# Expert weights loaded as two neighbouring rows per partition, with the contraction order permuted to match

## The chip, the cores and the metric

The kernel runs on one core of one Trainium2 chip. The metric is the device time of one execution in microseconds. Three runs of the kernel before took 1764.06, 1769.62 and 1772.02 us; the median is 1769.62 us.

## What is computed

Two layers of a diffusion block over 256 latent tokens and 256 context tokens of 1024 channels. Each layer is a dense part (RMSNorm, attention, convolution and pooling branches, gates, output projection) and then an expert part, which is what the change touches:

```python
def expert_choice_ffn(h, w_router, w_gate, w_up, w_down):
    B, N, _ = h.shape
    cap = (CAPACITY_FACTOR * N) // N_EXPERTS          # 32 tokens per expert
    aff = jax.nn.softmax(jnp.einsum('bnd,de->bne', h, w_router).astype(F32), axis=-1)
    g, idx = lax.top_k(jnp.transpose(aff, (0, 2, 1)), cap)
    xe = h[bidx, idx]
    a = jnp.einsum('becd,edf->becf', xe, w_gate)
    u = jnp.einsum('becd,edf->becf', xe, w_up)
    ye = jnp.einsum('becf,efd->becd', jax.nn.silu(a) * u, w_down) * g[..., None].astype(h.dtype)
    return jnp.zeros_like(h).at[bidx, idx].add(ye)
```

There are 16 experts per layer, each with three matrices of 1024 x 1024 in float32 (12 MB per expert, 192 MB per layer). Layer 0 runs the experts for both token sets, layer 1 for the latent tokens alone.

## The kernel before

A weight matrix of an expert comes in four tiles of 1 MB, each with 256 rows of the matrix, on 128 partitions: `t[p, k, :]` holds row `128 k + p` of the 256 (line 334, in `prefetch`). Each partition so gets two rows of 4 KB that lie 128 rows apart in memory. The last expert's down matrix is loaded in another cut: four tiles of 512 rows by half of the columns, in runs of 2 KB. `prefetch` takes the next tile of a fixed list (gate and up in turn, then down, expert by expert) and a free buffer from a fixed rotation (`slot`: 15 buffers in layer 0, 19 in layer 1, most of them taken over from the dense part), and issues the load on SP's DMA queue. All large weights go through that queue in program order; small operands such as the router's weights, 1024 runs of 64 bytes (line 839), go through ACT's queue.

The rows of a tile stand on the partitions, so that TensorE contracts over them: tile column `kk` of tile `i` needs the chosen tokens' features `128 k` to `128 k + 127`, with `k = 2 i + kk`. These come on the partitions by `gather` (line 988), a product of the tokens with a selection matrix in which 128 columns of the residual `XS` are the stationary operand. For the down product, the hidden values `hs` are transposed in the same chunks of 128 columns (line 1094). The router uses the same feature order: line 896 transposes `XS`, line 839 loads `w_router`, and the scale and shift (`A2`, `modT`) are transposed at lines 168 and 248.

Per expert, TensorE runs 64 instructions of gate and up (line 1079), the transposes of the hidden values (line 1094) and 32 of down (lines 1103 and 1108); every four experts (two in layer 1) follow the products that add the results back to the residual (line 1125).

In layer 1 the router's weights are issued at the end of the dense part, beside the first expert tiles that fill free buffers; line 842 scales them on GpSimd, and line 888 is the first product that uses them. What stands behind line 888 on TensorE waits with it.

Of the kernel before, what the change touches and what calls it, by code (L numbers as in the profile page):

```python
# [23 lines left out]
EPS = 1e-6  # L24
# per layer: conv taps issued per step of a section; engine of the low part of a split (v: DVE, p: GpSimd);
# engine that scales a head's probabilities; units per chunk of the modulation products
TAPS = dict(attn=(1, 4), pool=(4, 0), merge0=(8, 1), merge2=(9, 18))
# [11 lines left out]
def const_tables():  # L39
    """Tables that depend on shapes alone."""  # L40
    f = np.float32
    kc = np.zeros((128, KC_END), f)
    p = np.arange(128)
    kc[:, KC_ID:KC_ID + 128] = np.eye(128, dtype=f)
    kc[p ^ 16, KC_PERM + p] = 1.0
    kc[:, KC_U:KC_U + 128] = (p[:, None] <= p[None, :])
    kc[:, KC_MA:KC_MA + 128] = np.where(p[None, :] > p[:, None], f(-1e30), f(0))
    kc[:, KC_MB:KC_MB + 128] = np.where(p[None, :] < p[:, None], f(-1e30), f(0))
    kc[:, KC_IOTA:KC_IOTA + 32] = np.arange(1, 33)
    kc[:, KC_SCOL] = p % 32 + 1  # L50
    t = np.arange(SEQ)
    for g, w in enumerate(POOLW):
        cnt = np.clip(t + w - w // 2, 0, SEQ) - np.clip(t - w // 2, 0, SEQ)
        r = (f(w) / cnt.astype(f)).astype(f)
        kc[:, KC_EDGE + 16 * g:KC_EDGE + 16 * g + 8] = r[:8]
        kc[:, KC_EDGE + 16 * g + 8:KC_EDGE + 16 * g + 16] = r[-8:]
    row, col = (t // 64).astype(f), (t % 64).astype(f)
    fr = (f(10000.0) ** (-np.arange(16, dtype=f) / f(16))).astype(f)
    rope = np.zeros((128, 2, SEQ), f)
    for q in range(128):  # L60
        d = q % 64
        ang = (row if d < 32 else col) * fr[d % 16]
        sgn = f(-1.0) if (d // 16) % 2 == 0 else f(1.0)
        rope[q, 0] = np.cos(ang)
        rope[q, 1] = sgn * np.sin(ang)
    return kc, rope.reshape(128, 2 * SEQ)


@with_exitstack
def dit_block(ctx: ExitStack, tc: tile.TileContext, out, kc_in, rope_in, x, c, ctx_in, c_ctx,  # L70
# [38 lines left out]

# [1 line left out]
    gps = open_psum("psd0", mm=3, md=1, ax=4)  # L111
# [8 lines left out]
    ident = kc[:, KC_ID:KC_ID + 128]  # L120
    NV = 64
    misc = L.tile([128, 2048], F32, tag="ws", name="misc", bufs=2)
    kt = misc[:, 512:512 + KC_END - KC_U]
    vrow, crow = misc[0:NV, 0:128], misc[0:16, 128:256]

    def rows(ap):
# [3 lines left out]
    nc.sync.dma_start(crow[8:16], c_ctx.rearrange("(k p) -> k p", p=128))  # L130
    VN1, VN2, VCB, VLG, VLB, VPS = 0, 16, 32, 40, 48, 56
    nc.gpsimd.dma_start(kt, kc_in[:, KC_U:KC_END])
# [5 lines left out]
    tokens(0)  # L138
    for o, ap in ((VN1, norm1_g), (VN2, norm2_g), (VCB, conv_dw_b), (VLG, conv_ln_g),
                  (VLB, conv_ln_b), (VPS, pool_scale)):  # L140
        r = rows(ap)
        nc.sync.dma_start(vrow[o:o + r.shape[0]], r)
# [15 lines left out]
    ucat = P0.tile([128, 3, 128], BF16, name="ucat")  # L158
    vec = P0.tile([128, NV], F32, name="vec")

    def small_operands():
        pv2 = bank("ax")
        nc.vector.tensor_copy(identb, ident)
        nc.vector.tensor_copy(maskb, kt[:, KC_MA - KC_U:KC_MA - KC_U + 256].rearrange("p (a b) -> p a b", a=2))
        nc.vector.memset(ucat[:, 0, :], 0.0)
        nc.vector.tensor_copy(ucat[:, 1, :], kt[:, 0:128])
        nc.vector.memset(ucat[:, 2, :], 1.0)
        nc.tensor.transpose(pv2[:, 0:NV], vrow, ident[:NV, :NV])
        nc.vector.tensor_copy(vec, pv2[:, 0:NV])

# [8 lines left out]
    def rms_scale(ss, n):  # L179
        """(ss / DM + EPS) ** -0.5"""  # L180
        r = small([128, 2], "rstd")
# [4 lines left out]
    for l in range(DEPTH):  # L186
# [3 lines left out]

        # ================= dense part =================
        if l:
# [23 lines left out]
        def mod_group(ll, g):  # L216
# [30 lines left out]
            for b in range(4):  # L247
                nc.tensor.transpose(pt[:, b * 128:(b + 1) * 128], mr[:, b * 128:(b + 1) * 128], ident)
            ptv = pt.rearrange("p (b j s m) -> p s j b m", b=4, j=4, s=2)
# [38 lines left out]

# [1 line left out]
        order = ["x0", "x1", "x2", "x3"]  # L290
# [32 lines left out]
        def prefetch(n):  # L323
            for _ in range(n):
                w_e, e, i = next(seq)
                t = slot("we")
                if w_e is w_e_down and e == NE - 1:
                    h, kq = i // 2, i % 2
                    t = t.rearrange("p (k n) -> p k n", k=4)
                    src = w_e[l, e, 512 * kq:512 * (kq + 1), 512 * h:512 * (h + 1)]  # L330
                else:
                    t = t.rearrange("p (k n) -> p k n", k=2)
                    src = w_e[l, e, 256 * i:256 * (i + 1), :]
                nc.sync.dma_start(t, src.rearrange("(k p) n -> p k n", p=128))
                ahead.append(t)
# [5 lines left out]

# [1 line left out]
        xn = [half(f"A{s}", "xn").rearrange("p (t d) -> p t d", t=2) for s in range(2)]  # L343
# [12 lines left out]
        def mod_first(hf, tag):  # L356
            """shift and scale of the first norm, feature blocks 4 hf .. 4 hf + 3"""
            ps = bank(tag)
# [80 lines left out]
        def pump_mod(n=1):  # L439
            """advance the remaining modulation products by n chunks"""  # L440
            while n > 0:
# [33 lines left out]
        def mm3(ps, w, a, nk, n):  # L475
            """ps += w.T @ a over nk chunks of 128, each operand in two exact parts"""
            (wh, wl), (ah, al) = w, a
# [19 lines left out]

# [1 line left out]
        QS = DR.tile([128, NH, 256], F32R, tag="qf", name="QS")  # L499
# [17 lines left out]
        for u in range(2):  # L517
            tv = qw.pop() if qw else qload(u)
            for v in range(2):
# [5 lines left out]
                if NS == 2:  # L525
                    nc.scalar.activation(qx[:, 256:512], ps[:, 256:512], AF.Copy)
                # each head's rows: the leading part, and the rest on the other 64 partitions
                for kv in range(2):
# [28 lines left out]

# [1 line left out]
        def branch(name):  # L559
# [41 lines left out]
        def weigh(s, kv, pT, pr4, rs):  # L601
            """normalised probabilities, keys on the partitions"""
            nk = 4 if s == 0 else 2
# [31 lines left out]

# [1 line left out]
        W = 256 + 2 * CPAD  # L637
# [44 lines left out]

# [1 line left out]
        wp = DR.tile([128, 4, 128], F32, tag="k2", name="wp")  # L684
# [32 lines left out]

# [1 line left out]
        m = [half(f"A{i}", "m") for i in range(NS)]  # L719
# [46 lines left out]
        for g in range(4):  # L766
# [6 lines left out]
                                           op1=ALU.subtract)  # L773
# [1 line left out]
        def conv_norm():  # L775
# [51 lines left out]

        # ================= output projection, router, top-k =================
        tail[0] = True
# [8 lines left out]
        nc.gpsimd.memset(wr, 0.0)  # L838
        nc.scalar.dma_start(wr[:, :, 0:NE], w_router[l].rearrange("(k p) e -> p k e", p=128))
        wra = rt_[:, 256:256 + 256 * NS].rearrange("p (s k e) -> p s k e", s=NS, k=8)  # L840
# [44 lines left out]
        def route(s):  # L885
# [5 lines left out]
            for d2 in range(4):  # L891
                pt = bank("ax")
                for dd in range(2):
                    for t in range(2):
                        d = 2 * d2 + dd
                        nc.tensor.transpose(pt[:, dd * 256 + t * 128:dd * 256 + t * 128 + 128],
                                            XS[s][:, t, d * 128:(d + 1) * 128], ident)
                xT = t2("xT")
# [79 lines left out]

# [1 line left out]
        def gather(s, parts):  # L980
            ne = NE // parts
            for part in range(parts):
                es = slice(ne * part, ne * part + ne)
                for d in range(8):
                    px = bank("mm")[:, :32 * ne]
                    for t in range(2):
                        Sv = St[s][:, t, es].rearrange("p e c -> p (e c)")
                        nc.tensor.matmul(px, XS[s][:, t, d * 128:(d + 1) * 128], Sv, start=t == 0,  # L988
                                         stop=t == 1)
                    pxv = px.rearrange("p (e c) -> p e c", e=ne)  # L990
# [36 lines left out]

        # ================= experts =================
        GE = 4 if NS == 2 else 2
        REP = 128 // GE  # L1030
        nsq = [small([128, 2, 2], "nsq") for _ in range(NS)]
        for e in range(NE):
# [3 lines left out]
            if e % GE == GE - 1:  # L1036
                # scatter matrices of the group: (expert, slot) by token, scaled by the affinity
                sgs = []
# [25 lines left out]

            # gate and up: column tiles of the array side by side
            nb = 2 if NS == 2 else 1
# [24 lines left out]
            for f in range(nb):  # L1091
                for q in range(4):
                    o = 256 * f + 64 * q
                    nc.tensor.transpose(pt[:, o:o + 64], hs[f][0:64, 128 * q:128 * q + 128],  # L1094
                                        ident[0:64, 0:64])
            hT = t2("hT")
# [106 lines left out]
```

## Time and profile before

| | |
|---|---|
| median of 3 runs | 1769.62 us |
| profiled execution, first to last instruction (span) | 1765.2 us |
| time of the profiled execution beside its span | the page lists none; its span stands within the three runs |
| TensorE busy | 1537.8 us (87%) |
| VectorE, ScalarE, GpSimd busy | 668.7, 407.7, 236.1 us |
| moved by DMA | 529.94 MB, mean 300 GB/s |
| SP's DMA queue | 179472 packets, 526.25 MB, 78.4% of 16 engines' span |
| expert loads | 3 x 128 transfers of 1024 KB |

The page cuts the span into 40 slices of 44.1 us. A packet is what one DMA engine moves in one piece: one contiguous run, at most. The share of a queue is the time that its packets took, over 16 engines and the span; over 100% means that packets of one engine overlap a little. TensorE's busy time is modelled, so a high share does not show that it sets the pace.

### The profile page before, as it was taken

The numbers are of one execution on the slowest core, as the hardware profiler recorded it, in microseconds if no ns is written. First come the engines' busy times: TensorE is split into PE (matmuls) and PEld (weight loads), VectorE is DVE, ScalarE is ACT, GpSimd is POOL, SyncE is SP. The second block draws the span as 40 slices with busy tenths as digits, with TensorE's granted clock in tenths as the row PEclk, the third lists the DMA queues.
The fourth block names the chain that finished last, engine by engine and source line by source line (L and its number), as shares of the span: only waits on it lengthen the run. The fifth ranks groups of instructions, "written<-read, shape, count | busy, mean of one in ns | idle before, by whom it ended". The sixth has DMA issues, their size and how long they took to land.

```text
span 1765.2 us, 19600 instructions
## 1 busy us (share of the span) xinstructions
PE 1537.8 (87%) x7792; PEld 809.1 (46%) x7792; DVE 668.7 (38%) x1144; ACT 407.7 (23%) x760; POOL 236.1 (13%) x242
## 2 busy tenths in 40 slices
PE   5999989999989999898899899999978766667676
PEld 2665566888654433232333267789742111111111
DVE  2568993452551221121211278965532110111011
ACT  2455312232431100000000157434421000000001
POOL 1300430154730000000000020225100000000000
PEclk9999999999999999999999999999989888888888
DMA  9733536254638999999999845666799999999996
GB/s 307 270 126 127 166 108 232 78 180 146 218 120 334 409 409 409 408 409 409 409 409 409 319 178 173 215 232 207 297 364 409 409 409 409 409 409 409 409 409 248
DMA packets 184331, 529.94 MB, mean 300 GB/s; under 512 B 11768, under 2 KB 60352, under 8 KB 179120
## 3 DMA queue, kind: packets, MB, share of 16 engines
q1 hardware_dynamic: 179472, 526.25, 78.4%
q10 hardware_dynamic: 4096, 1.97, 0.4%
q8 instruction: 61, 1.00, 0.2%
q0 software_dynamic: 672, 0.47, 0.1%
q14 instruction: 30, 0.25, 0.0%
HBM read 527.60 MB, written 1.05 MB: 299 GB/s over the span
## 4 chain that ended last, share of the span: by engine, by line
PE 37%; DMA 27%; DVE 5%; ACT 2%; POOL 2%; issue 1%; SPq 0%; POOLq 0%; ACTq 0%; DVEq 0%
DMA we<-in_w_e_up_dram 22%; PE mm L1079 11%; PE mm L1103 5%; DMA we<-in_w_e_down_dram 3%; PE mm L1108 3%; PE mm L480 2%; PE mm L988 2%; PE mm L479 2%; PE mm L482 2%; PE ax L1125 2%; PE mm L873 2%; DMA rt<-in_w_router_dram 1%; DVE hm L1086 1%; DVE acc L461 1%; PE ax L1094 1%
## 5 line engine op out<-in xcount | busy, mean ns | idle before, releaser
L1079 PE MATMUL mm<-we,xeT 128*64 128x512 f32 (+1 forms) x2048 | 445.9, 656 | 95.6 <-DMA we<-in_w_e_up_dram 75.3
L1079 PEld LDWEIGHTS mm<-we,xeT 128*64 128x64 f32 (+1 forms) x2048 | 126.6, 129 | 405.6 <-issue 201.1
L479 PE MATMUL mm<-hh,ws 128*128 128x512 f32 (+1 forms) x672 | 223.3, 351 | 1.4 <-ACT hh L413 1.2
L480 PE MATMUL mm<-hl,ws 128*128 128x512 f32 (+1 forms) x672 | 220.8, 347 | 0.0
L1086 DVE TENSOR_TENSOR hm<-si,mm 64x512 f32<-64x512 f32 x48 | 33.1, 690 | 468.1 <-ACT si L1084 467.2
L212 ACT ACTIVATE ws<-w 128x1024 fp32r<-128x1024 f32 x132 | 139.1, 1057 | 273.3 <-PE mm L482 186.2
L1084 ACT ACTIVATE si<-mm 64x512 f32<-64x512 f32 x48 | 28.4, 591 | 751.1 <-PE mm L1079 751.1
L461 DVE SCALAR_TENSOR_TENSOR acc<-up,dw,acc 128x512 f32<-128x512 f32 (+1 forms) x240 | 154.5, 687 | 0.9
L213 DVE TENSOR_TENSOR ws<-w,ws 128x1024 fp32r<-128x1024 f32 x94 | 123.6, 1319 | 71.9 <-ACT ws L212 71.5
L479 PEld LDWEIGHTS mm<-hh,ws 128*128 128x128 f32 x672 | 129.1, 193 | 31.5 <-issue 10.7
L480 PEld LDWEIGHTS mm<-hl,ws 128*128 128x128 f32 x672 | 129.2, 193 | 18.1 <-DVE hl L414 2.4
L1103 PE MATMUL mm<-we,hT 128*64 128x512 f32 x512 | 128.8, 635 | 8.4 <-ACT hT L1098 8.4
L482 PE MATMUL mm<-hh,ws 128*128 128x512 f32 (+1 forms) x672 | 134.8, 341 | 0.5 <-DVE ws L213 0.4
L213 POOL TENSOR_TENSOR ws<-w,ws 128x1024 fp32r<-128x1024 f32 x38 | 96.2, 2537 | 213.4 <-ACT ws L212 177.5
L482 PEld LDWEIGHTS mm<-hh,ws 128*128 128x128 f32 x672 | 107.6, 190 | 17.7 <-issue 2.4
L1044 POOL COPY sg<-kc 48x128 f32<-48x128 f32 (+1 forms) x16 | 4.4, 286 | 774.6 <-PE ax L1125 773.5
L1108 PE MATMUL mm<-we,hT 128*32 128x512 f32 x512 | 87.5, 790 | 11.9 <-DMA we<-in_w_e_down_dram 8.2
L1115 DVE TENSOR_TENSOR Y<-mm,G 32x512 f32<-32x512 f32 x64 | 44.0, 687 | 138.5 <-PE mm L1103 137.8
L1103 PEld LDWEIGHTS mm<-we,hT 128*64 128x64 f32 x512 | 39.2, 145 | 88.5 <-issue 75.1
L1125 PE MATMUL ax<-Y,sg 128*128 128x512 f32 x128 | 60.6, 619 | 8.8 <-DVE Y L1118 6.4
L1118 DVE TENSOR_TENSOR Y<-mm,G 64x512 f32<-64x512 f32 x32 | 22.0, 689 | 91.9 <-PE mm L1108 91.5
L749 POOL TENSOR_TENSOR m<-m,th 128x512 f32<-128x512 f32 (+1 forms) x32 | 36.6, 1143 | 145.1 <-DVE th L747 145.0
(271 smaller groups left out, 1594.6 us busy)
## 6 DMA issues: line engine op xcount, KB each, us to landing
we<-in_w_e_gate_dram SPq DMA_DIRECT2D x128, 1024.0 KB, 18.2
we<-in_w_e_up_dram SPq DMA_DIRECT2D x128, 1024.0 KB, 18.3
we<-in_w_e_down_dram SPq DMA_DIRECT2D x128, 1024.0 KB, 18.3
w<-in_w_mod_dram SPq DMA_DIRECT2D x40, 1024.0 KB, 5.0
w<-in_w_in_dram SPq DMA_DIRECT2D x38, 1024.0 KB, 5.2
w<-in_w_out_dram SPq DMA_DIRECT2D x12, 1024.0 KB, 5.1
w<-in_w_mod_dram SPq DMA_DIRECT2D x16, 512.0 KB, 10.8
w<-in_w_in_dram SPq DMA_DIRECT2D x8, 512.0 KB, 12.1
```

What stands on the lines that cost most here:

```text
L212: nc.scalar.activation(h, src, AF.Copy)
L213: (nc.gpsimd if eng == "p" else nc.vector).tensor_sub(lw, src, h.bitcast(F32))
L461: nc.vector.scalar_tensor_tensor(acc[:, ch], up[:, ch, :, k:k + 256], dw[:, 4 * k + ch:4 * k + ch + 1], acc[:, ch], op0=ALU.mult, op1=ALU.add)
L479: nc.tensor.matmul(ps, wh[:, k, :], ah[:, k, :n], start=k == 0, stop=False)
L480: nc.tensor.matmul(ps, wh[:, k, :], al[:, k, :n], start=False, stop=False)
L482: nc.tensor.matmul(ps, wl[:, k, :], ah[:, k, :n], start=False, stop=k == nk - 1)
L1079: nc.tensor.matmul(o, xeT[k // 4][:, k % 4, e, :], w[:, kk, 512 * f:512 * f + 512], start=k == 0, stop=k == 7)
L1086: nc.vector.tensor_mul(hm[0:64, :], si[0:64, :], pgu[f][64:128, :])
L1103: nc.tensor.matmul(pd[64 * h:64 * h + 64, :], hT[:, 64 * k:64 * k + 64], rhs, start=k == 0, stop=k == 7)
L1108: nc.tensor.matmul(pd[o:o + 32, :], hT[:, c0:c0 + 32], rhs, start=k < 2, stop=k >= 6)
L1115: nc.vector.tensor_mul(Y[b0:b0 + 32, s, cols], pd[rw, :], G2[l][rw, :])
L1125: nc.tensor.matmul(po, sgs[s][:, t * 128:(t + 1) * 128], Y[:, s, cols], start=True, stop=True)
```

## The change

Tile `t` of an expert's matrix now holds rows `2 p` and `2 p + 1` of its 256 rows on partition `p`: one run of 8 KB per partition, contiguous in memory and in the buffer, and the whole tile is 1 MB in one piece. Chunk `c` of 128 features is then no longer the columns `128 c` to `128 c + 127`, but every second column of a block of 256 (`paired(c)`), and all that meets such a chunk follows: the gathers, the router's transposes and weights, the transposes of the hidden values, and the scale, shift and gain of the second norm. These read their 128 columns with a step of two elements. The last expert's down matrix keeps its runs of 2 KB and is issued as eight loads of 512 KB instead of four of 1 MB. The router's weights are issued as two loads instead of one, with the same 1024 runs of 64 bytes.

```diff
+def paired(c):
+    return slice(256 * (c // 2) + c % 2, 256 * (c // 2) + 256, 2)
...
-    NV = 64
+    NV = 48
...
+    n2row = misc[0:8, 256:512]
...
+    nc.sync.dma_start(n2row, norm2_g.rearrange("l (i c) -> (l i) c", c=256))
...
-        nc.vector.tensor_copy(vec, pv2[:, 0:NV])
+        for kk in range(2):
+            nc.tensor.transpose(pv2[:, NV + 8 * kk:NV + 8 * kk + 8], n2row[:, paired(kk)], ident[:8, :8])
+        nc.vector.tensor_copy(vec[:, 0:NV], pv2[:, 0:NV])
+        nc.vector.tensor_copy(vec[:, VN2:VN2 + 16].rearrange("p (i k) -> p k i", k=2),
+                              pv2[:, NV:NV + 16].rearrange("p (k i) -> p k i", k=2))
...
             for b in range(4):
-                nc.tensor.transpose(pt[:, b * 128:(b + 1) * 128], mr[:, b * 128:(b + 1) * 128], ident)
+                cols = paired(b) if g else slice(b * 128, (b + 1) * 128)
+                nc.tensor.transpose(pt[:, b * 128:(b + 1) * 128], mr[:, cols], ident)
...
                 if w_e is w_e_down and e == NE - 1:
                     h, kq = i // 2, i % 2
                     t = t.rearrange("p (k n) -> p k n", k=4)
-                    src = w_e[l, e, 512 * kq:512 * (kq + 1), 512 * h:512 * (h + 1)]
+                    for ii in range(2):
+                        r0 = 512 * kq + 256 * ii
+                        nc.sync.dma_start(t[:, 2 * ii:2 * ii + 2], w_e[
+                            l, e, r0:r0 + 256, 512 * h:512 * (h + 1)].rearrange("(p k) n -> p k n", k=2))
                 else:
                     t = t.rearrange("p (k n) -> p k n", k=2)
-                    src = w_e[l, e, 256 * i:256 * (i + 1), :]
-                nc.sync.dma_start(t, src.rearrange("(k p) n -> p k n", p=128))
+                    nc.sync.dma_start(t, w_e[l, e, 256 * i:256 * (i + 1), :].rearrange(
+                        "(p k) n -> p k n", k=2))
...
-        nc.scalar.dma_start(wr[:, :, 0:NE], w_router[l].rearrange("(k p) e -> p k e", p=128))
+        for kk in range(2):
+            nc.scalar.dma_start(wr[:, kk::2, 0:NE], w_router[l].rearrange(
+                "(i p k) e -> p k i e", p=128, k=2)[:, kk])
...
-                                            XS[s][:, t, d * 128:(d + 1) * 128], ident)
+                                            XS[s][:, t, paired(d)], ident)
...
-                        nc.tensor.matmul(px, XS[s][:, t, d * 128:(d + 1) * 128], Sv, start=t == 0,
-                                         stop=t == 1)
+                        nc.tensor.matmul(px, XS[s][:, t, paired(d)], Sv, start=t == 0, stop=t == 1)
...
-                    nc.tensor.transpose(pt[:, o:o + 64], hs[f][0:64, 128 * q:128 * q + 128],
-                                        ident[0:64, 0:64])
+                    nc.tensor.transpose(pt[:, o:o + 64], hs[f][0:64, paired(q)], ident[0:64, 0:64])
```

SP's queue at the end of layer 1, where the last expert's tiles are issued (`we` is an expert tile, `xo` the result). Before:

```order
L334 DMA we<-in_w_e_gate_dram 128x2x1024
L334 DMA we<-in_w_e_up_dram 128x2x1024
L334 DMA we<-in_w_e_down_dram 128x4x512 x4
L1172 DMA out_dram<-xo 128x512 x4
L1199 UNCONDITIONAL_BRANCH
```

and changed:

```order
L348 DMA we<-in_w_e_gate_dram 128x2048
L348 DMA we<-in_w_e_up_dram 128x2048
L344 DMA we<-in_w_e_down_dram 128x2x512 x8
L1187 DMA out_dram<-xo 128x512 x4
L1214 UNCONDITIONAL_BRANCH
```

The order of the tiles is the same all through; a gate, up or down tile is one run per partition, and the last down matrix takes eight issues.

ScalarE's queue in layer 1 at the end of the dense part (`mh` is the leading half of the merged branches, `rt` the router's weights, `gb` a gate, `ws` a split weight). Before:

```order
L823 ACTIVATE mh<-m 128x256 x4
L839 DMA rt<-in_w_router_dram 128x8x16
L855 ACTIVATE gb<-ax 128x512 x2
L212 ACTIVATE ws<-w 128x1024 x4
L881 ACTIVATE junk,ssq<-xr 128x512
```

and changed:

```order
L838 ACTIVATE mh<-m 128x256 x4
L855 DMA rt<-in_w_router_dram 128x4x16 x2
L872 ACTIVATE gb<-ax 128x512 x2
L223 ACTIVATE ws<-w 128x1024 x4
L898 ACTIVATE junk,ssq<-xr 128x512
```

Here the two router loads stand together in the place of the one. In layer 0 the second of them stands behind one split (line 223) and one tanh (line 750).

## Rows read from the trace of the kernel before

**Rows 1.** The page: DMA's busy tenths and rate in 40 slices.
```profile
DMA  9733536254638999999999845666799999999996
GB/s 307 270 126 127 166 108 232 78 180 146 218 120 334 409 409 409 408 409 409 409 409 409 319 178 173 215 232 207 297 364 409 409 409 409 409 409 409 409 409 248
```
**Rows 2.** The page: the chain that ended last, by line.
```profile
DMA we<-in_w_e_up_dram 22%; PE mm L1079 11%; PE mm L1103 5%; DMA we<-in_w_e_down_dram 3%; PE mm L1108 3%; PE mm L480 2%; PE mm L988 2%; PE mm L479 2%; PE mm L482 2%; PE ax L1125 2%; PE mm L873 2%; DMA rt<-in_w_router_dram 1%; DVE hm L1086 1%; DVE acc L461 1%; PE ax L1094 1%
```
**Rows 3.** The chain in order of time: start us, us, what.
```profile
531.54 13.88 PE mm L1079 x64
...
684.39 19.84 DMA we<-in_w_e_up_dram
...
1297.65 7.00 PE mm L1079 x64
...
1349.00 18.31 DMA we<-in_w_e_up_dram
```
**Rows 4.** Busy time by stretch: PE, PEld, DVE, ACT, POOL, PEclk, DMA share, GB/s.
```profile
540.00:970.00 430.00, 398.01 (x1700) 148.38 (x1697) 86.19 (x134) 36.11 (x66) 1.58 (x6) 0.98 1.02 408
1305.00:1735.00 430.00, 313.64 (x1656) 80.63 (x1655) 59.07 (x93) 25.16 (x53) 2.61 (x8) 0.87 1.03 409
```
**Rows 5.** SP's own timeline, layer 1's experts: start us, us, instruction.
```profile
1410.55 2.31 SPq L334 DMA_DIRECT2D we<-in_w_e_up_dram  x1
```
**Rows 6.** DMA from 700 to 900 us, experts' 4 KB runs: packets, MB, share.
```profile
q1 hardware_dynamic: 21181, 81.66, 102.3%
```
**Rows 7.** DMA from 1039 to 1044 us, 8 KB runs of w_mod: packets, MB, share.
```profile
DMA packets 288, 2.04 MB, mean 407 GB/s; under 512 B 29, under 2 KB 30, under 8 KB 49
q1 hardware_dynamic: 288, 2.04, 99.5%
```
**Rows 8.** As rows 4, a stretch inside two w_mod tiles.
```profile
43.00:46.00 3.00, 2.81 (x35) 1.13 (x34) 0.12 (x1) 0.00 (x0) 0.00 (x0) 1.00 0.99 415
```
**Rows 9.** As rows 4, early in layer 0's experts.
```profile
555.00:565.00 10.00, 10.00 (x50) 3.31 (x48) 2.74 (x4) 0.00 (x0) 0.00 (x0) 1.00 0.99 369
```
**Rows 10.** The chain at the router's load, layer 1.
```profile
1251.44 14.92 DMA rt<-in_w_router_dram
```
**Rows 11.** PE's timeline there, with its idle time before and the releaser.
```profile
1266.49 0.65 PE L888 MATMUL ax<-modT,rt 128*32 128x128 f32 x16 [1.51 <-DMA rt<-in_w_router_dram]
```
**Rows 12.** DMA from 1256 to 1264 us: SP's queue (q1), ACT's (q10).
```profile
q1 hardware_dynamic: 801, 3.08, 98.0%
q10 hardware_dynamic: 801, 0.05, 7.4%
```
**Rows 13.** SP's timeline from 1243 to 1275 us, the expert tiles.
```profile
1243.56 0.37 SPq L334 DMA_DIRECT2D we<-in_w_e_up_dram  x1
...
1249.30 0.47 SPq L334 DMA_DIRECT2D we<-in_w_e_gate_dram  x1
...
1264.65 0.37 SPq L334 DMA_DIRECT2D we<-in_w_e_down_dram  x1
...
1274.09 0.37 SPq L334 DMA_DIRECT2D we<-in_w_e_down_dram  x1
```
**Rows 14.** As rows 4, behind the router's load.
```profile
1270.00:1275.00 5.00, 5.00 (x29) 3.91 (x22) 1.22 (x1) 1.06 (x1) 0.00 (x0) 1.00 0.20 77
```
**Rows 15.** Weight loads, min/median/max ns: the router's transposes and the gathers.
```profile
L896 PEld LDWEIGHTS ax<-kc,xr x32: 137/140/143, 463.4 to 1280.1; 128*128 128x128 f32 x32
L896 PEld LDWEIGHTS ax<-kc,xc x16: 138/140/143, 497.8 to 513.1; 128*128 128x128 f32 x16
L988 PEld LDWEIGHTS mm<-S,xr x160: 186/192/333, 508.4 to 1327.9; 128*128 128x128 f32 x160
L988 PEld LDWEIGHTS mm<-S,xc x128: 186/192/192, 527.7 to 601.1; 128*128 128x128 f32 x128
```
**Rows 16.** The same of line 853, one column of the identity read 128 times.
```profile
L853 PEld LDWEIGHTS ax<-GM,kc x12: 185/188/192, 444.1 to 1250.3; 128*128 128x128 f32 x12
```
**Rows 17.** The router's tile: issue to landing in layer 0.
```profile
DMA to landing us min/median/max: 2.2/2.2/2.2
```

More of the change, by code (lines that the diff above doesn't have):

```diff
@@ L130, in dit_block @@
     nc.sync.dma_start(crow[8:16], c_ctx.rearrange("(k p) -> k p", p=128))
-    VN1, VN2, VCB, VLG, VLB, VPS = 0, 16, 32, 40, 48, 56
+    VN1, VCB, VLG, VLB, VPS, VN2 = 0, 16, 24, 32, 40, 48
     nc.gpsimd.dma_start(kt, kc_in[:, KC_U:KC_END])
@@ L138, in dit_block @@
     tokens(0)
-    for o, ap in ((VN1, norm1_g), (VN2, norm2_g), (VCB, conv_dw_b), (VLG, conv_ln_g),
+    nc.sync.dma_start(n2row, norm2_g.rearrange("l (i c) -> (l i) c", c=256))
+    for o, ap in ((VN1, norm1_g), (VCB, conv_dw_b), (VLG, conv_ln_g),
                   (VLB, conv_ln_b), (VPS, pool_scale)):
@@ L158, in dit_block @@
     ucat = P0.tile([128, 3, 128], BF16, name="ucat")
-    vec = P0.tile([128, NV], F32, name="vec")
+    vec = P0.tile([128, NV + 16], F32, name="vec")
     def small_operands():
```

## The prediction

> **What bounds the kernel now.** I read the 40 slices first. DMA stands at 9 tenths and 409 GB/s over slices 13 to 21 and 30 to 38 [rows 1]: two plateaus, with the dense parts before and between them. The chain by line puts 22% and 3% of the span on expert tiles in flight [rows 2]. In order of time the reader should see where each plateau takes over: the experts' first products start at 531.54 us in layer 0 and 1297.65 us in layer 1, and run on tiles fetched earlier; the chain turns to a tile in flight at 684.39 and at 1349.00 us [rows 3]. In the stretches 540 to 970 and 1305 to 1735 us the 16 engines are full (share 1.02 and 1.03) at 408 and 409 GB/s [rows 4]. TensorE looks busy in the first of them, 398 of 430 us, but that time is modelled and stretched by late tiles. SP needs 2.31 us to get rid of one issue there [rows 5], about the time in which one tile of 1.0486 MB flows (2.56 us at 409 GB/s): it is held by its own full queue. So each plateau ends when its last tile has landed, and lasts tiles times the time per tile.
>
> **The change, part by part.**
>
> *Runs of 8 KB.* The price of a run is in the DMA queue's rows. With 4 KB runs, 81.66 MB in 200 us at 102.3% of 16 engines are 1.023 x 16 x 200 / 81.66 = 40.09 engine-us per MB [rows 6]. The nearest rows for 8 KB runs are the loads of `w_mod`, which already have such runs: 2.04 MB in 5 us at 99.5% are 39.02 engine-us per MB [rows 7], 2.7% less. Taken to the plateau, a tile goes from 2.567 us (1.0486 MB at 408.5 GB/s) to 2.498 us, 0.069 us saved. The plateaus hold 430 x 408 / 1048.6 = 167 and 430 x 409 / 1048.6 = 168 tiles [rows 4], together 335: **-23.1 us**. The ends: the same `w_mod` stretch, taken by its plain rate, shows 407 GB/s [rows 7], so no gain at all, though its edges are not full; a shorter one shows 415 GB/s at a share of 0.99 [rows 8], which is 0.99 x 16 / 0.415 = 38.17 engine-us per MB, 4.8% less, 0.123 us per tile, -41 us. I take the longer stretch and its share, because it has the most bytes and corrects for engines that stood idle.
>
> The Trainium skill speaks for and against here (HBM Reference, Specifications): it gives a core about 358 GB/s of its memory, by which longer runs could bring nothing. The trace shows 409 GB/s held [rows 4], above that, so that share is not what binds here. The same page puts a core streaming alone at about 425 GB/s, bound by its DMA engines; by that ceiling the estimate would be 2.467 us per tile and -33 us.
>
> *Early in layer 0* the engines are not always fed: from 555 to 565 us the rate is 369 GB/s [rows 9], because SP waits until TensorE has freed a buffer. Faster tiles wait more there. The stretch lost 10 x (409 - 369) / 409 = 1.0 us; I allow as much once more: **+1 us** (0 to 2).
>
> *The router's load in layer 1* is what the longer runs can harm. It goes through ACT's queue, and takes 14.92 us [rows 10], against 2.2 us in layer 0, where no expert tiles flow [rows 17]. In the 8 us from 1256 the two queues moved 801 packets each [rows 12]: the engines take one from each in turn, so that each 64 byte run waits for one 4 KB run, 8 x 16 / 801 = 0.160 us. The load has 1024 runs, 64 per engine: 10.2 us. Beside 8 KB runs a turn would be 0.160 x 2 x 0.973 = 0.311 us, and 64 of them 19.9 us, 9.7 us more. But the expert tiles run out first: six are issued from 1243.56 to 1249.30 us, three more by 1264.65, the next only at 1274.09 [rows 13], and from 1270 to 1275 us the rate is 77 GB/s [rows 14]. With nine tiles at 2.50 instead of 2.57 us, SP's queue is empty at about 1269.5, and what is left of the router's load then lands within about half a microsecond: 1270.0 instead of 1266.4 us, +3.6. TensorE already waits 1.51 us for this load [rows 11], so all of it shows, and the wait lies before 1297.65, where the buffers of the second plateau begin to come free. **+3.5 us**, ends 0 (the load gets through as now) and +9.7 (the queue does not run dry). Cutting the load in two adds one issue on ACT, off the path while TensorE is still at the output projection; in layer 0 no expert tiles flow beside it and it stands far ahead of its use. Nothing for both.
>
> *Columns with a step of two.* All of them are stationary operands, so the cost would be in weight loads: 48 for the router at 0.140 us, 288 for the gathers at 0.192 us [rows 15], and 192 hidden-value transposes and 16 of the scale and shift. The last two lie in the plateaus or beside other products. On the path, before buffers come free, are the router's 48 and some 96 of the gathers (64 ahead of the experts' start at 531.54 us, 32 ahead of 1297.65, as the program orders them). The same number of columns is loaded, so I see no gain. The nearest row is a load that reads one column 128 times, step 0: 0.188 us [rows 16], as much as one with neighbouring columns [rows 15]. I take 0; the other end is a doubled load, 48 x 0.140 + 96 x 0.192 = +25 us.
>
> *Small edits.* Two more transposes and one more copy for the second norm's gain, near the start, on the path: each of the kind that takes 0.1 to 0.2 us in the rows above, **+0.3 us** (0 to 1). The last down matrices stay at 2 KB runs; eight issues instead of four hide behind SP's full queue: 0, ends -1 and +0.5. Expert by expert the order on SP is the same, so nothing jumps a queue.
>
> **Sum:** -23.1 + 1 + 3.5 + 0.3 = -18.3 us. Against the profiled span of 1765.2 us that is 1746.9; the median of the runs, 1769.62, is 4.4 us above that span, and 1769.6 - 18.3 = **1751.3 us** is my forecast. What is late next is still DMA: at 2.50 us per tile an expert takes 30.0 us, and TensorE's own work per expert is some 26 us in layer 0: the 152.9 us from 531.54 to 684.39, in which it sets the pace [rows 3], hold nearly six experts.
>
> **The rivals.**
>
> 1. *The rate stays* at 409 GB/s, because something other than the run's length sets it, the memory or the write into the buffers. For it: the plain 407 GB/s of rows 7. Against it: the share beside that rate. Only the costs remain: 1769.6 + 3.8 = 1773.4 us, no measurable change.
> 2. *The rate rises more*, to what rows 8 show: 1769.6 - 41 + 4.8 = 1733 us.
> 3. *The router's load waits out the whole of its turns*, since SP's queue, which holds more tiles of half as many runs, does not run dry: +6.2 us on the forecast, 1757.5 us.
> 4. *Loads with a step of two take longer.* The place is the router and the gathers before each plateau. Doubled, +25 us undo the gain: 1751.3 + 25 = 1776 us, no change; the point from which it decides is a load 2.1 times as long, and at three times the kernel is slower, 1801 us. For it: no row has a load with a step of two. Against it: step 0 costs nothing extra [rows 16].
>
> That the change does not do what it says, I set aside: the rows of SP's new order show one run of 2048 elements per partition.
>
> **How the numbers follow.** Forecast 0.62, rival 1 0.12, rival 2 0.06, rival 3 0.12, rival 4 0.08 (0.03 of it near a doubled load, 0.05 beyond). A measurement of this kernel can tell about 0.5% from no change, 8.8 us: below 1760.8 is faster, above 1778.4 slower. Faster: the forecast, rivals 2 and 3 less a little for their upper ends, 0.76. Same: rival 1, half-way cases and part of rival 4, 0.18. Slower: the rest of rival 4 and a rate that falls, 0.06. The range is 1738 (a gain per tile of 0.11 us) to 1766 (0.03 us and the router's upper end): it leaves out rivals 1, 2 and 4 for the most part, some 0.2.
>
> **What would show it.** Plateaus at about 420 GB/s instead of 409; SP's issues on the plateaus no longer held 2.3 us each, and longer times to landing, since twice as many tiles fit its queue; the router's load at 18 to 19 us and TensorE's wait for it at about 5 us; the weight loads of the gathers still at 0.19 us. I am wrong if the plateau's rate has not moved, or if layer 1's first expert products do not start earlier than 1297.65 us: they should start at about 1291, with 167 x 0.069 = 11.5 us from the first plateau less 4.8 us of costs.

## The result and the profile after

The changed kernel takes **1751.26 us** (median of 4 runs, 1748.18 to 1752.59); the kernel before, 4 runs, 1767.67 us. The ratio is 0.9911, with a 95% interval of 0.9895 to 0.9927: faster by 0.9%. The forecast was 1751.3 us.

The page of the changed kernel, DMA and rate in 40 slices, the chain that ended last by line, and the issues of expert tiles (x count, KB each, us to landing):

```profile
DMA  9833537244637999999999845776689999999996
GB/s 307 274 127 126 163 107 238 78 166 149 223 138 282 422 421 421 420 421 421 421 420 421 302 177 174 230 239 206 248 334 420 421 421 421 421 421 421 421 421 245
...
DMA we<-in_w_e_up_dram 25%; DMA we<-in_w_e_down_dram 13%; PE mm L1095 7%; PE mm L1118 4%; PE mm L495 2%; PE mm L494 2%; PE mm L497 2%; PE mm L1005 2%; PE mm L890 2%; DMA rt<-in_w_router_dram 1%; DMA w<-in_w_in_dram 1%; POOL ws L224 1%; PE ax L1140 1%; PE md L244 1%; PE ax L643 1%
...
we<-in_w_e_up_dram SPq DMA_DIRECT2D x128, 1024.0 KB, 19.8
```

Both plateaus stand where they stood, at 421 GB/s, not 409 [rows 1]. DMA from 700 to 900 us, the stretch of [rows 6] (packets, MB, share of 16 engines):

```profile
q1 hardware_dynamic: 11542, 84.05, 101.1%
```

Half the packets for more bytes: 1.011 x 16 x 200 / 84.05 = 38.49 engine-us per MB, against 40.09.

Then the chain in order of time (start us, us, what), for [rows 3] and [rows 10]:

```profile
532.54 13.88 PE mm L1095 x64
...
986.88 9.74 DMA w<-in_w_in_dram
...
1239.97 20.01 DMA rt<-in_w_router_dram
1260.03 1.07 PE ax L905 x14
...
1294.88 7.00 PE mm L1095 x64
```

These places cut the span into stages. The first load of `w_in` that the chain shows behind the first plateau began at 997.48 us before. The columns on the right are experiments that are told below; the products that first use the router's weights stand at line 905 here and 888 before.

| us | before | after | runs only | steps only | router early | before, router early |
|---|---|---|---|---|---|---|
| layer 0's experts start | 531.54 | 532.54 | 532.48 | 533.06 | 532.17 | 533.15 |
| from there to that `w_in` load | 465.94 | 454.34 | 454.06 | 464.39 | 455.39 | 464.81 |
| router's issue to landing | 14.92 | 20.01 | 20.75 | 14.73 | off the path | off the path |
| router's first product starts | 1266.49 | 1260.03 | 1260.44 | 1265.64 | 1252.84 | 1264.81 |
| from there to layer 1's experts | 31.16 | 34.85 | 34.68 | 32.54 | 31.49 | 31.24 |
| from there to the end | 467.55 | 455.82 | 453.98 | 467.72 | 456.27 | 467.55 |
| span | 1765.2 | 1750.7 | 1749.1 | 1765.9 | 1740.6 | 1763.6 |

From before to after the two plateaus give 11.6 + 11.7 us. The span falls by 14.5 us, so some 9 of these 23 us are lost elsewhere: 1.0 ahead of layer 0's experts, 5.1 in the router's load and 3.6 from its landing to layer 1's experts; the stretch up to its issue is 0.9 us shorter. TensorE's timeline there, with the idle time before and its releaser:

```profile
1253.40 0.38 PE L905 MATMUL ax<-modT,rt 128*32 128x128 f32 x2 [0.32 <-DMA rt<-in_w_router_dram]
1260.03 1.07 PE L905 MATMUL ax<-modT,rt 128*32 128x128 f32 x14 [6.25 <-DMA rt<-in_w_router_dram]
```

It waits 6.57 us, not 1.51 [rows 11]. Busy time by stretch, with the columns of [rows 4]; PEclk is the one behind the bracket of POOL:

```profile
1250.00:1255.00 5.00, 3.46 (x16) 2.37 (x14) 4.56 (x6) 3.46 (x6) 0.00 (x0) 1.00 1.06 410
1255.00:1260.00 5.00, 0.00 (x0) 0.00 (x0) 0.48 (x1) 0.00 (x0) 0.00 (x0) 0.84 0.51 205
1260.00:1265.00 5.00, 4.97 (x28) 3.96 (x29) 0.69 (x1) 0.60 (x1) 0.62 (x1) 0.50 0.00 0
...
1275.00:1280.00 5.00, 4.09 (x19) 2.14 (x19) 1.73 (x3) 1.90 (x5) 1.38 (x4) 0.66 1.01 428
```

TensorE was idle from 1253.8 to 1260.0 us; the granted clock then stood at half, 1.2 GHz, for the router's first products, which took 421 ns at the median and 272 before (count, then ns min/median/max; before first):

```profile
L888 PE MATMUL ax<-modT,rt x16: 269/272/297, 1266.5 to 1266.9; 128*32 128x128 f32 x16
L905 PE MATMUL ax<-modT,rt x16: 270/421/421, 1253.4 to 1260.7; 128*32 128x128 f32 x16
```

It fell again from 1275 us on; before, the same work lies between 1279 and 1284 us, with the clock at 1.00.

Weight loads from 460 to 600 us (xcount | busy us, mean ns), where [rows 15] had 140 and 192 ns:

```profile
L1005 PEld LDWEIGHTS mm<-S,xr 128*128 128x128 f32 x32 | 5.8, 196 | 4.7 <-issue 4.6
...
L913 PEld LDWEIGHTS ax<-kc,xr 128*128 128x128 f32 x16 | 2.3, 207 | 2.5 <-POOL xr L897 1.3 <-DVE xr L897 0.8 <-issue 0.4
```

A step of two costs a gather's load 4 ns, but a transpose's load 67 ns.

### The profile page after: what moved, and what is told of

The parts are those of the page before. It is cut to its first block, busy times and chain, and to the rows that moved or that the text cites. A ratio compares the mean times of both kernels' runs of the same rounds, so it can differ in the third digit from the quotient of the medians.

```text
span 1750.7 us, 19617 instructions
## 1 busy us (share of the span) xinstructions
PE 1533.1 (88%) x7794; PEld 825.5 (47%) x7794; DVE 668.5 (38%) x1145; ACT 408.1 (23%) x760; POOL 235.3 (13%) x242
## 4 chain that ended last, share of the span: by engine, by line
DMA 39%; PE 27%; DVE 3%; POOL 2%; ACT 1%; issue 1%; POOLq 0%; ACTq 0%; SPq 0%; DVEq 0%
DMA we<-in_w_e_up_dram 25%; DMA we<-in_w_e_down_dram 13%; PE mm L1095 7%; PE mm L1118 4%; PE mm L495 2%; PE mm L494 2%; PE mm L497 2%; PE mm L1005 2%; PE mm L890 2%; DMA rt<-in_w_router_dram 1%; DMA w<-in_w_in_dram 1%; POOL ws L224 1%; PE ax L1140 1%; PE md L244 1%; PE ax L643 1%
## 5 line engine op out<-in xcount | busy, mean ns | idle before, releaser
L1095 PE MATMUL mm<-we,xeT 128*64 128x512 f32 (+1 forms) x2048 | 424.3, 628 | 86.7 <-DMA we<-in_w_e_up_dram 65.8
L1118 PE MATMUL mm<-we,hT 128*64 128x512 f32 x512 | 132.9, 652 | 8.4 <-ACT hT L1113 8.4
L1110 PE MATMUL ax<-kc,hm 64*128 64x64 f32 x192 | 32.1, 290 | 29.2 <-DVE hm L1102 28.9
## 6 DMA issues: line engine op xcount, KB each, us to landing
we<-in_w_e_gate_dram SPq DMA_DIRECT2D x128, 1024.0 KB, 19.8
we<-in_w_e_up_dram SPq DMA_DIRECT2D x128, 1024.0 KB, 19.8
we<-in_w_e_down_dram SPq DMA_DIRECT2D x120, 1024.0 KB, 19.8
```

The costliest lines, as they stand in the source:

```text
L1095: nc.tensor.matmul(o, xeT[k // 4][:, k % 4, e, :], w[:, kk, 512 * f:512 * f + 512], start=k == 0, stop=k == 7)
L1118: nc.tensor.matmul(pd[64 * h:64 * h + 64, :], hT[:, 64 * k:64 * k + 64], rhs, start=k == 0, stop=k == 7)
```

## The experiments

The theory: the whole gain is the length of the runs, a fixed cost per run in a DMA engine; what was given back is the router's load, whose runs now wait for longer ones, and the slower clock behind the wait. Rivals: the gain is the order in memory; the lost 3.6 us are the stepped columns; the router lands later for another reason than turns.

### The runs alone, the steps alone

Runs alone, on the kernel before:

```diff
-                nc.sync.dma_start(t, src.rearrange("(k p) n -> p k n", p=128))
+                    nc.sync.dma_start(t, w_e[l, e, 256 * i:256 * (i + 1), :].rearrange(
+                        "(p k) n -> p k n", k=2))
```

(and the last down matrix as in the change.)

> The kernel before with the 8 KB runs of the expert tiles alone (and the last down projection's two pieces): contiguous columns everywhere, the router loaded by one transfer as before. Its output is not the reference's, since the hidden rows of a tile no longer meet the columns that they belong to. Theory 1 (the whole gain is the length of the runs; the router's load pays because each of its runs of 64 B waits out a run of a tile): both plateaus at about 421 GB/s, the router lands after 19 to 21 us and its first use waits 5 to 7 us, as in the change. The split of what the change gave back: if the 3.6 us that it lost between that landing and layer 1's first experts come from TensorE's lower granted clock after the wait, they are lost here too (34 to 35 us, time near 1750); if they come from the stepped columns they are not (31 to 32 us, time near 1746). Rival (the stepped columns cost nothing and the two-part router transfer causes the longer load): the router lands after about 15 us and the time is near 1742.

Steps alone: the change with the old line for the tiles put back.

> The change with the expert tiles loaded as before (4 KB runs, rows 128 apart), everything else as in the change; its output is not the reference's, since the tiles' rows no longer meet the permuted columns. Theory 1: plateaus at 408 to 410 GB/s, router load back at 14 to 16 us in spite of its two transfers, weight loads of the router's transposes 190 to 230 ns. The time is then that of the kernel before plus the stepped columns alone: 1768 to 1769 if the 3.6 us after the router's landing came from the clock, 1771 to 1773 if they came from the steps. Rival (two transfers make the router late): landing 19 us or more, time near 1773 with a PE wait of 5 us or more.

**Measured.** Runs alone: 1751.14 us (1749.86 to 1754.22), ratio to the kernel before 0.9922 (0.9897 to 0.9946), the change's own time. Steps alone: 1765.59 us, where the kernel before on that chip took 1764.74 (the 1768 to 1769 that was expected stood on 1767.67); ratio 1.0003 (0.9992 to 1.0014), nothing. DMA from 700 to 900 us, runs alone:

```profile
q1 hardware_dynamic: 11546, 84.07, 101.1%
```

and steps alone:

```profile
q1 hardware_dynamic: 21189, 81.68, 102.3%
```

The rate goes with the runs. So does the router: with one transfer it takes 20.75 us beside long runs, with two transfers 14.73 beside short ones, so the split is not the cause. And the time behind its landing is 34.68 us with long runs and *contiguous* columns: the loss there isn't the steps'. The granted clock of runs alone at the place of the wait:

```profile
1255.00:1260.00 5.00, 0.00 (x0) 0.00 (x0) 0.48 (x1) 0.00 (x0) 0.00 (x0) 0.53 0.64 242
1260.00:1265.00 5.00, 4.56 (x29) 3.71 (x30) 0.69 (x1) 0.60 (x1) 0.61 (x1) 0.50 0.00 0
```

Steps alone took 32.54 us there, 1.4 more than before, with a clock of 0.87 and 0.78 from 1275 to 1285 us; in the comparison of times that doesn't show.

### Same place in memory, other runs

One tile by two transfers, a row of each pair at a time, against the change:

```diff
-                    nc.sync.dma_start(t, w_e[l, e, 256 * i:256 * (i + 1), :].rearrange(
-                        "(p k) n -> p k n", k=2))
+                    src = w_e[l, e, 256 * i:256 * (i + 1), :].rearrange("(p k) n -> p k n", k=2)
+                    for kk in range(2):
+                        nc.sync.dma_start(t[:, kk], src[:, kk])
```

> The change with each tile fetched by two transfers, one per row of the pair: the same 1 MB of neighbouring memory and the same place on the chip, but runs of 4 KB and twice the transfers. Theory 1 (a fixed cost per run): 408 to 410 GB/s in the plateaus, that is 23 us more than the change there, less the router's 5 us and a part of the 3.6 us: 1766 to 1772. Rival (what helps is that a partition's data lie together and the tile is read in one sweep, not the run's length): 419 to 421 GB/s and, since the router's turns are those of 4 KB runs again, 1743 to 1748.

And by halves of the columns, `t[:, :, 512 * h:512 * h + 512]` for `h` 0 and 1:

> The change with each tile fetched by two transfers, one per half of the columns: the same pair of rows in a partition, but runs of 2 KB. Theory 1 (each run costs a DMA engine a fixed time beside its bytes): 40.08 engine-us per MB at 4 KB and 38.49 at 8 KB give 13 ns a run and 36.9 us per MB, so 43.3 engine-us per MB at 2 KB; with the share of 1.02 to 1.04 that the engines showed, 377 to 385 GB/s in the plateaus, and a time of 1830 to 1850. Rival a (only runs over 4 KB are better, all below alike): 407 to 410 GB/s, 1764 to 1770. Rival b (short runs break the stream): below 360 GB/s.

**Measured.** Runs of 4 KB from neighbouring rows: 1764.26 us, ratio 0.9996 (0.9983 to 1.0008): the gain is gone, though each tile is still 1 MB in one piece. The row of 700 to 900 us:

```profile
q1 hardware_dynamic: 22432, 81.69, 102.4%
```

That is the rate of the kernel before. Order in memory falls as a cause, and so does the number of transfers: this kernel issues twice as many as the kernel before and holds the same rate, and the one with runs of 2 KB, below, issues as many as this one and holds less. The time came 2 us under what was expected, because the router's load was off the path altogether, not just 5 us shorter. Runs of 2 KB, the kernel executed once: 1812.96 us, and

```profile
q1 hardware_dynamic: 40056, 77.22, 104.5%
```

1.045 x 16 x 200 / 77.22 = 43.3 engine-us per MB, the number expected from the 4 and 8 KB runs by a fixed 13 ns per run. These engine-us count packets that overlap twice, and the shares stand 1.1, 2.3 and 4.5% over full at 8, 4 and 2 KB. By elapsed time, 16 x 200 us over the same bytes, the three are 38.1, 39.2 and 41.4 per MB: again on one line, at some 9 ns per run, and that is what the plateaus pay. The rate, 387 GB/s, is a little over the 377 to 385 expected, and the time is 17 us under the range: I had forgotten that shorter runs free the router's load. With it, 335 tiles x (1.0486/387 - 1.0486/421) = 73 us less 10.5 us at the router is 62.8, on 1751.3 some 1814.

The depth of the queue shows here too. A tile lands 19.8 us after its issue in the change, and half a tile 10.2 us:

```profile
we<-in_w_e_gate_dram SPq DMA_DIRECT2D x256, 512.0 KB, 10.2
```

Eight transfers each: 8 x 2.49 and 8 x 1.28 us.

### The router's load

Half as many runs at the same place, in layer 1, against the change:

```diff
+        if last:
+            wraw = MO.tile([128, 128], F32, name="wraw")
+            nc.scalar.dma_start(wraw.rearrange("p (i m) -> p i m", i=4), w_router[l].rearrange(
+                "(i p k) e -> p i (k e)", p=128, k=2))
+            nc.gpsimd.tensor_copy(wr[:, :, 0:NE], wraw.rearrange("p (k e) -> p k e", k=8))
```

> The change with layer 1's router fetched at the same place in the program, but by one transfer of 512 runs of 128 B (32 for each DMA engine, not 64) into a plain tile, and spread into place by a copy on GpSimd. Theory 1 (one run of the router for one run of a tile): 32 turns of 0.311 us are 10 us, with what a landing takes beside that 11 to 13.5 us; PE needs the router 13.9 us after the issue (in the change: 20.01 less 6.57, plus 0.46 between the two issues), so the wait is 0 to 0.5 us, the granted clock stays at 1.00 behind it, and the time is 1740 to 1743, as with the early load. Rival (the router's transfer waits for the tiles that were issued before it, whose landing takes 19.8 us too): the landing stays at 19 to 21 us, the wait at 5 to 7 us, the time at 1750 to 1752.

The same load moved up beside that of `wp`, at 1001.1 us, some 235 us earlier, with its tile in a pool that lives through layer 1:

> The change with layer 1's router weights fetched early, in runs of 128 B, beside the pooling weights while the queues are not full, and copied into place on GpSimd. Theory 1: the wait of 6.6 us before the router's first use is gone, with it the half-speed stretch behind it; plateaus unchanged at 421 GB/s. If the 3.6 us after the landing are the clock's: from the router's first use to layer 1's first experts 31 to 32 us and the time near 1741 to 1743. If they are the steps': 34 to 35 us, time near 1744 to 1746. Rival (the wait ends together with another one, the tiles' own issue, so removing it frees nothing): 1749 to 1752.

And the early load on the kernel before, with its own feature order:

> The kernel before with layer 1's router weights fetched early, beside the pooling weights, and copied into place on GpSimd; 4 KB runs throughout. Theory 1: before, the router cost only PE's wait of 1.51 us and the granted clock was 1.00 behind it, so 1 to 2 us are gained, a time of 1762.5 to 1764. Then the 10 us that the early load gained on the change are all what the longer runs had given back at this place. Rival (the router's load costs the tiles bandwidth or delays the slots, whatever the runs): 5 us or more are gained, 1760 or less.

**Measured.** 512 runs: 1743.68 us (1742.55 to 1746.61), ratio 0.9876 (0.9861 to 0.9890). The chain at the place:

```profile
1239.04 14.07 DMA wraw<-in_w_router_dram
1253.23 0.47 POOL rt L858
1253.74 0.65 PE ax L911 x16
```

It landed half a microsecond later than expected, and with the copy behind it TensorE still waited 1.2 us; but the tiles in flight took 19.8 us as before, so the load does not stand behind them. DMA from 1244 to 1248 us in the change, SP's queue and ACT's:

```profile
q1 hardware_dynamic: 232, 1.64, 98.5%
q10 hardware_dynamic: 231, 0.01, 4.1%
```

One for one, as in [rows 12]. 4 x 16 / 231 = 0.277 us a turn.

Early load: 1740.63 us (1739.37 to 1742.55), ratio 0.9860 (0.9840 to 0.9879). The wait is gone, and with it the slow clock. The chain,

```profile
1252.84 0.58 PE ax L914 x16
...
1284.33 7.00 PE mm L1104 x64
```

and the clock of the same stretch:

```profile
1250.00:1255.00 5.00, 5.00 (x40) 3.98 (x39) 4.72 (x6) 3.46 (x6) 0.00 (x0) 1.00 1.00 411
1255.00:1260.00 5.00, 5.00 (x29) 3.53 (x27) 1.60 (x3) 1.66 (x2) 0.00 (x0) 1.00 0.45 180
```

From the first product to the experts it is 31.49 us against 34.85 in the change, with the same stepped columns. 2.3 of these 3.4 us lie in the first six microseconds (1260.03 to 1266.28 in the change, 1252.84 to 1256.76 here, up to the same product of the output projection), at the half clock behind the wait. The rest, 28.60 against 27.57 us, is not shown to follow from the wait: in the kernel with runs of 4 KB from neighbouring rows TensorE does not wait for the router at all, and yet the rest takes 28.54 us, with the same second fall of the clock,

```profile
1275.00:1280.00 5.00, 3.67 (x16) 1.85 (x16) 2.21 (x3) 1.93 (x5) 1.95 (x5) 0.66 0.99 377
```

and what brings that fall about is open. 0.3 us (31.49 less 31.16) are left for the steps. With 512 runs the whole stretch took 33.2 us, at a granted clock of 0.86 from 1265 to 1270 us, so with the same steps it varies by 1.7 us. On the kernel before the early load gives 1763.90 us against 1765.76, ratio 0.9993 (0.9979 to 1.0006), and moves layer 1's experts by 1.6 us. Of the 10.5 us that it moves them in the change, some 9 are thus a price of the longer runs. This version, the change with the early load, is the fastest of all: its interval lies wholly under the change's.

### A step of four

```diff
+def quad(c):
+    return slice(512 * (c // 4) + c % 4, 512 * (c // 4) + 512, 4)
...
-                                            XS[s][:, t, paired(d)], ident)
+                                            XS[s][:, t, quad(d)], ident)
```

(and so in the gathers and the transposes of `hs`.)

> The change with a step of four in place of two in the columns of the router's and the hidden values' transposes and of the gathers, everything else alike; it computes something else, as those columns no longer belong to the rows of the weights. It measures the loads of stationary operands: 0.140 us for neighbouring columns and 0.21 us for every second one in the transposes, 0.192 and 0.196 us in the gathers. If what counts is how many 16-byte lines a load touches: 0.28 to 0.42 us in the transposes and over 0.25 us in the gathers. If any step costs the same: 0.20 to 0.22 and 0.19 to 0.20 us. The Trainium skill's page SBUF - State Buffer, Partition Mapping to AXI Ports, says both that two hits on a line of 16 bytes are needed and that a step of 4 is free for fp32; by the second of these the transposes would stand at 0.14 us with a step of two, which the change's 0.21 us contradict. The time is within 4 us of the change's in any case.

**Measured.** Weight loads from 460 to 600 us:

```profile
L1010 PEld LDWEIGHTS mm<-S,xr 128*128 128x128 f32 x32 | 9.3, 312 | 2.7 <-issue 0.4
...
L918 PEld LDWEIGHTS ax<-kc,xr 128*128 128x128 f32 x16 | 2.3, 207 | 2.5 <-POOL xr L902 1.3 <-DVE xr L902 0.8 <-issue 0.4
```

The two kinds differ. The gathers' loads go 192, 196, 312 ns for steps of 1, 2 and 4; the transposes' 140, 207, 207. Neither theory holds for both. The time, 1765.85 us in a single execution, is 14.6 us above the change's: the bound of 4 us was wrong. The chain shows where,

```profile
530.60 7.73 PE mm L1010 x32
538.34 13.88 PE mm L1100 x64
...
998.84 10.65 DMA w<-in_w_in_dram
```

as layer 0's experts start 5.8 us later, and the plateau ends 12.0 us later than in the change. 96 more gathers stand between its first experts, where TensorE sets the pace and frees the buffers; a block of 32 takes 7.7 us there, not 4.0. The rest is layer 1's gathers, 7.73 us for the last 32 before the experts against some 5.4.

The Trainium skill (SBUF - State Buffer; the sentence stands in "Door 1: The DMA port swizzle", not in the section that the expectation names) asks for two hits on each 16-byte line, and also calls a step of 4 free for fp32. For the gathers the first agrees, 196 and 312 ns, and the second doesn't; for the transposes, which pay at two and no more at four, neither does.

## Why the prediction was right, and where it was off

- **Runs of 8 KB, -23.1 us.** Right in mechanism; that the size is right too owes something to luck. The plateaus gave 11.6 + 11.7 = 23.3 us; the price is 38.49 engine-us per MB, not the 39.02 taken from `w_mod`. Put into the prediction's own step, which carries the ratio of the two prices over to the tile, 38.49 against 40.09 would have given -34 us. The step leaves out that the share falls as well, from 102.3 to 101.1%; the wrong price and the missing share made up for each other. By elapsed time a tile became 2.9% cheaper, where 2.7% was forecast. The cause is shown: 4 KB runs from the same place lose the gain, and 2 KB runs follow the same line. Rival 1 (the rate stays) and rival 2 (-41 us) fall. The ceiling of about 425 GB/s that the Trainium skill gives (HBM Reference, Specifications) agrees with 421; its share of 358 does not bind here.
- **Early in layer 0, +1 us.** Not told apart. Rows 9's stretch slowed to 338 GB/s from 369, but the whole plateau shortened as forecast. Layer 0's experts start 1.0 us later, and 1.6 us later in a kernel that changes nothing ahead of them (the early router on the kernel before), so a difference of 1 us there can't be told from scatter. The small edits' 0.3 us can't be seen either.
- **The router's load, +3.5 us.** The mechanism was right, the term was mis-sized: the load took 5.1 us longer, 20.0 and not 18 to 19, and TensorE waited 6.57 and not 5 us. I had SP's tiles running dry and the rest of the load landing within half a microsecond. The gap came, and let 333 packets through in one microsecond, but not the last ones: 21 packets were left at 1256 and took until 1259.4, some three per us until the last. DMA from 1254 to 1255 and from 1258 to 1259 us, ACT's queue:

```profile
q10 hardware_dynamic: 333, 0.02, 22.9%
```
```profile
q10 hardware_dynamic: 3, 0.00, 0.2%
```

  That is the pace of a single engine that still takes its turns. In the trace's packet records they come, but for one pair, about 0.32 us apart up to 1259.37, from 1258.1 on each just as an 8 KB packet of 0.31 us ends; when no 8 KB packet is left, the last nine follow within 0.07 us. Why one engine was behind is open. Rival 3's full 64 turns beside tiles would have been 24.6 us. "All of it shows" was also short by what stands behind a wait: **2.3 us at the lower granted clock**, which the sum put at nothing. That is the step that failed. Some 1.3 us more, 3.7 in all against the kernel before, came with the later fall of the clock, whose cause is open. Together they are why the experts began at 1294.88 and not at 1291 us, and why the profiled span fell by 14.5 and not 18.3 us.
- **Columns with a step of two, 0.** Right for the time (steps alone, 1.0003), wrong for the reason. "As much as one with neighbouring columns" holds for the gathers, 196 ns, but the transposes' loads are half as long again; 48 of them on the path, at 0.067 us and partly beside products, are at most 3.2 us. Step 0 was no guide to step 2. Rival 4's mechanism is real: at a step of two for the transposes, where it cost nothing that the times show, and at four for the gathers.
- **SP's issues.** No longer held for 2.31 us [rows 5] but for 0.33, as forecast, and the landing is longer, 19.8 us. But "twice as many tiles fit its queue" was wrong: eight transfers are under way, and each issue waits for the landing of an earlier one. The waits of SP's queue from 1350 to 1700 us (us in total, times, longest):

```profile
SPq L348 <- DMA we<-in_w_e_up_dram: 100.3, 47, 3.6
SPq L348 <- DMA we<-in_w_e_gate_dram: 98.5, 47, 2.2
SPq L348 <- DMA we<-in_w_e_down_dram: 98.5, 47, 2.2
```

- **The total.** The median hit owes something to chance. The terms are off by 3.8 us in the span (1746.9 forecast, 1750.7 measured). The base was 1769.62, a median 4.4 us above the span of another execution; the execution profiled after took only 1.9 us more than its own span, and the medians of the kernel before, with later runs, are 1767.67, 1764.74 and 1765.76 us. The two errors, +3.8 and -2.5 us, nearly cancel, and the median of the change lies 1.3 us under its profiled execution. The upper end of the range, as it is explained (0.03 us per tile and +9.7 us at the router), adds up to 1770.6 and not 1766 us.

## What to carry to other kernels

A stream that holds all 16 engines full is priced per run as well as per byte: two sizes of run in one's own traces give both parts, and the third size can be forecast; take the parts from elapsed time, since overlapping packets make the packets' own time too long. Before lengthening the runs of such a stream, look for small transfers of many runs on another queue that TensorE needs while it flows: they pay turn by turn, and moving one out of the stream's way gave here 10 us, nearly half of what the longer runs gave. And price a wait of TensorE with what it does to the granted clock behind it.

## What the runs showed of the hardware that was not expected

- A run costs a DMA engine some 13 ns of packet time beside its bytes: 38.49, 40.08 and 43.3 engine-us per MB at 8, 4 and 2 KB. By elapsed time it is some 9 ns: 38.1, 39.2 and 41.4.
- Two queues take turns run by run: 232 packets of SP's queue and 231 of ACT's in 4 us. The Trainium skill (DMA: Bandwidth & Descriptors, Queues, rings and completion order) has an engine drain a packet of some 9 to 17 descriptors from one queue before it turns to the other. The trace contradicts it for these loads: the last engine's 64 byte packets begin at 1258.11, 1258.43, 1258.74 and 1259.05 us, with a single 8 KB packet between each two. The counts alone would not show it, as equal packets on both queues give equal counts too.
- A wait of 6.25 us was followed by a granted clock of 0.50 for 5 us, and the products there took 421 ns and not 272; right behind waits of 1.2 to 1.5 us it stayed at 1.00.
- Of two kinds of fp32 loads of 128 columns, the transposes' go from 140 to 207 ns at a step of two and stay there at four; the products' stay at 196 and go to 312. Why they differ is open.
